# Hybrid attention block on one Trainium2 core: builds of x's combinations placed earlier, their writes placed behind the next weights, half of p and u kept in SBUF

## The chip, the cores and the metric

The kernel runs on one core of a Trainium2 chip. The metric is the device time of one execution in microseconds (us), the lower the better. The kernel before takes 834.61 us, the median of three runs (834.24, 834.61 and 836.61).

A core has five engines with their own instruction queues, each worked off in order: TensorE (PE, matmuls into PSUM; PEld are its weight loads), VectorE (DVE), ScalarE (ACT), GpSimd (POOL) and SyncE (SP, which here only issues DMAs). SBUF is the memory on the chip, HBM the one beside it.

## What is computed

x has 512 positions of 2048. One projection `h @ w_in` gives everything; two attention groups follow, and one output projection.

```python
h = _rmsnorm(x, norm_g[l])
proj = h @ w_in[l]
(qa, kca, vca, ksa, vsa, kwa, vwa, za, ga, qb, kb, vb, zb) = jnp.split(proj, offsets, axis=-1)
kc = _compress(_rope(_heads(kca, N_KV_A, HEAD_DIM_A)), cmp_k_pos[l], cmp_k_w1[l], cmp_k_w2[l])
vc = _compress(_heads(vca, N_KV_A, HEAD_DIM_A), cmp_v_pos[l], cmp_v_w1[l], cmp_v_w2[l])
...
o_a = gates[..., 0:1] * o_cmp + gates[..., 1:2] * o_sel + gates[..., 2:3] * o_win
y_a = o_a.reshape(B, S, WIDTH_A) * jax.nn.silu(za)
...
x = x + jnp.concatenate([y_a, y_b], axis=-1) @ w_out[l]
return _rmsnorm(x, final_g)
```

Group A has 8 heads of 128 on two key heads, with a compressed, a selected and a window branch; `_compress` takes blocks of 32 positions, adds a position table and runs a two-layer network over each block. Group B has 16 heads of 64 with a window and sinks.

## The kernel before, in words

Every float32 operand is split in a high part (ACT, a copy to fp32r) and a low part (DVE, the rest), and every product is three matmuls, high x high, high x low, low x high (`mm3`, L111 to L114). x stays in SBUF so split (xh, xl: 16 row tiles of 128 x 512).

Weights come in units of 512 KB or less: `load_unit` (L80) issues the load on SP into one of three buffers (raw0 to raw2; the compression weights cw have two of their own), ACT makes whi (L88), DVE wlo (L89), each in a ring of three. A load waits for the wlo three units back, a split for PE's last use three units back.

A planner of the build, with its own model of times, orders each engine's queue; `tc.issue_after(...)` in the source ties an instruction behind another one, such as the last wlo (`last["lo"]`) or the last load of weights (`last["dma"]`).

The stages, in order of time:

1. Start to 52 us: the first half of w0 (keys and values to be compressed), x loaded and split beside it.
2. 52 to 96: the second w0 loop (L291), 8 units of 24 matmuls. Beside it DVE scales the results (`kv_evac`, L199), and makes the blocks to be compressed (`blocks_part`, L210: ff on DVE, L214; high part on ACT, L215; low part on DVE, L216), which go to two tiles F0 and F1.
3. 96 to 126: the w1s loop (L324), 8 times 24 matmuls of w1s (`tok_chunk`) and 8 that compress keys with F0 and a unit of cw (`compress_unit`).
4. 126 to about 176: the w2s loop (L361), the same with 408 columns and F1 for values. `k_evac` (L312) finishes two of the keys in each of these loops, `v_evac` (L333) the values behind them.
5. The q tile and then the z tile of head 0 (`proj`, L369, 48 matmuls each), the evacuation of values and gates (L385 to L396), the compressed values VC (L397 to L409), then `p0.close()` (L410): the memory of the first stages, s0, s0b and rawc, goes to the pool wk of the heads (among it raw3, a fourth buffer for weights, and the tile that q is evacuated to).
6. To about 480: heads 0 to 7 of group A. From head 1 on q and z are made as a pair (`pair`, L614) by Strassen's scheme on 2 x 2 blocks, seven products of 24 matmuls of 256 columns in place of eight. The weights come in four quarters (wq) and are added on DVE (L624). On x's side the scheme needs combinations of its quarters.
7. Then group B, and the output projection.

The combinations of x are made once. Eight times `build` (L267, for the pair of row tiles m) takes two rows of x that `rows(m)` (L262) has loaded anew, combines their quarters (one ACT and four DVE steps, L272 to L276), and splits four forms f (four ACT, four DVE steps, L279 and L280): f = 0 is p, 1 is u, 2 is q, 3 replaces a quarter of x. All go to HBM, to fd, with one 1 MB write for each m (L282). SP issues it where it stands in the queue, and waits there for the build. The rows stand in one buffer of two halves, stage[0], the forms in stage[1]; both lie in the memory of the values (V), and from m = 4 on in that of F0 (`both`, L341).

One build is in the second w0 loop (behind unit 6), three in the w1s loop (0, 2, 5), four in the w2s loop (1, 2, 4, 6). `forms_back` (L584) loads it all back behind the first quarters of wq: eight loads for the tiles pu0 to pu7 (p and u, high and low, m below 4 and from 4), four that swap forms f = 3 into the even row tiles of x (`swap_x`; the old content was copied to xd at L303), four for f = 2 into the places of group 1's keys and values, which wait in HBM (Kd, Vd).

Of the kernel before, what the change touches and what calls it, by code (L numbers as in the profile page):

```python
# [34 lines left out]
def hybrid_block(ctx, tc, xT, xtm, w0, w1s, w2s, wz, wq, wkb, wo0, wos, cw1, cw2, cpos, rope, tabs, sinks, gT, fg, out):  # L35
# [27 lines left out]
    fd = dram("fd", 4, 2, P, KT // 2, 256)  # L63
# [41 lines left out]
    stage = [kv.tile([P, 2048], F32, name=f"st{e}", tag=f"V{e}") for e in "HL"]  # L105
# [15 lines left out]

    p0 = ExitStack()
    s0 = p0.enter_context(sb("s0"))
    vbs = s0.tile([P, NQ, P], F32, name="vbs")
# [33 lines left out]
    sqa = s0.tile([P, S], F32, name="sqa")  # L158
# [36 lines left out]
    kvts = [s0.tile([P, 2, S + 16], F32, name=f"kvt{b}") for b in range(2)]  # L195
# [11 lines left out]
    def blocks_tile(b):  # L207
        return s0.tile([P, 32, P], F32R, name=f"F{b}", tag=f"F{b}")

    def blocks_part(Fb, b, g, half):  # L210
        ff = tmp("ff").rearrange("p (a b) -> p a b", b=32)
        js = slice(half * 16, half * 16 + 16)
        src = kvts[b][:, g, half * 16:half * 16 + S].rearrange("p (b j) -> p j b", j=16)
        dve.tensor_tensor(out=ff, in0=src, in1=pos[:, b, js].unsqueeze(2).to_broadcast([P, 16, 32]), op=ALU.add)  # L214
        act.activation(Fb[:, js, g * 32:g * 32 + 32], ff, AF.Copy)  # L215
        dve.tensor_tensor(out=Fb[:, js, 64 + g * 32:96 + g * 32], in0=ff,  # L216
                          in1=Fb[:, js, g * 32:g * 32 + 32].bitcast(F32), op=ALU.subtract)

    def compress_unit(Fb, b, u, acc):
        hi, lo = load_unit(cw1[:, b, u], 1024, rawc)  # L220
        for j in range(4):
            jj = 4 * u + j
            cs = slice(j * 256, j * 256 + 256)
            pe.matmul(acc[:, 0:256], Fb[:, jj, :], hi[:, cs], start=jj == 0, stop=False)
            pe.matmul(acc[:, 0:256], Fb[:, jj, :], lo[:, cs], start=False, stop=jj == 31)
# [33 lines left out]
    even = [x.rearrange("p (m e) s -> p e m s", e=2)[:, 0, :, 0:256].bitcast(F32) for x in (xh, xl)]  # L259
    todo = []  # L260

    def rows(m):  # L262
        xr = stage[0][:, (m % 2) * 1024:(m % 2) * 1024 + 1024].rearrange("p (e s) -> p e s", e=2)
        nc.sync.dma_start(xr, xT[:, 2 * m:2 * m + 2, :])
        todo.append((m, xr, stage[1].rearrange("p (f c) -> p f c", f=8)))

    def build():  # L267
        m, xr, ft = todo.pop(0)
        ge, go = [gt[:, 2 * m + e:2 * m + e + 1] for e in range(2)]
        a11, a21, a12, a22 = xr[:, 0, H0], xr[:, 0, H1], xr[:, 1, H0], xr[:, 1, H1]  # L270
        with tc.issue_after(last["lo"]), tc.issue_after(last["hi"]):
# [5 lines left out]
            for f, (src, scale) in enumerate(((a11, 1.0), (a12, -1.0), (a21, ge), (a22, 1.0))):  # L277
                hi, lo = [ft[:, 2 * f + e, :].bitcast(F32R) for e in range(2)]
# [8 lines left out]
    bp = [lambda Fb=Fb, b=b, g=g, half=half: blocks_part(Fb, b, g, half)  # L287
          for b, Fb in enumerate((F0, F1)) for half in range(2) for g in range(2)]
    work = [kv[:1], kv[1:2], kv[2:], bp[0:2], bp[2:4], bp[4:5], bp[5:7], bp[7:]]
    acc1 = [bank(4 + i) for i in range(4)]  # L290
    for u in range(KT // 2):  # L291
# [12 lines left out]
        if u == 6:  # L304
            build()
# [34 lines left out]
    VH, VL = [kvp.tile([P, 2, NQ, 2, P], F32R, name=f"V{e}", tag=f"V{e}") for e in "HL"]  # L340
    both = s0.tile([P, 4096], F32, name="both", tag="F0")  # L341
    stage[:] = both[:, 0:2048], both[:, 2048:4096]
    with tc.issue_after(last["dma"]):
        rows(4)
        rows(5)
# [10 lines left out]

    for t in range(NQ):
# [11 lines left out]
    def proj(src, odd_first=False):  # L369
        ps = psp.tile([P, S], F32, name="pj", tag="pj")  # L370
        ready = []
        for u in range(2):
            ready.append(load_unit(src[:, u], 1024))
            ks = range(8 * u, 8 * u + 8)
            if odd_first:
                ks = [k for par in (1, 0) for k in range(par, KT, 2)] if u else []
            for k in ks:
                hi, lo = ready[k // 8]
                js = slice((k % 8) * P, (k % 8) * P + P)
                mm3(ps, hi[:, js], lo[:, js], xh[:, k, :], xl[:, k, :], k == (1 if odd_first else 0),  # L380
                    k == (KT - 2 if odd_first else KT - 1))
        return ps

    q0 = proj(wz[0])
    for t in range(NQ):  # L385
        v_evac(t, 1, sacc2[t])
        act.activation(vbs[:, t, :], sacc2[t][:, 256:384], AF.Copy, scale=rstd[:, t:t + 1])
        dve.tensor_scalar(gates[:, t, :], sacc2[t][:, 384:408], rstd[:, t:t + 1], None, op0=ALU.mult)
    for e in range(2):
        nc.sync.dma_start(Kd[e], (KH, KL)[e][1].bitcast(F32))  # L390
        nc.sync.dma_start(Vd[e], (VH, VL)[e][:, 1].rearrange("p t w c -> p (t w c)").bitcast(F32))
# [875 lines left out]
```

## Time and profile before

| | us |
|---|---|
| median of three runs | 834.61 |
| the profiled execution | 838.46 |
| its span, first to last instruction | 836.7 |
| PE busy | 815.8 |
| DVE busy | 665.9 |
| ACT busy | 486.4 |
| POOL busy | 86.8 |

The granted clock of TensorE is 0.997 on the mean. The DMA engines move 132.49 MB, at a mean of 158 GB/s. An instruction counts as busy from start to end, and PE's matmuls overlap: one starts before the last one's results are written. So idle time between matmuls is real, while a busy PE may still be slower than it could be. In a timeline the bracket behind a row has the idle time of the engine just before it, and the instruction or DMA whose end released it. Times within the span are counted from its start.

### The profile page before, as it was taken

To read this page: it belongs to the slowest core of one execution; us is meant where nothing else is said; L and a number is where in the kernel's file an instruction comes from. 1 tells how busy PE (TensorE), PEld (TensorE's weight loads), DVE (VectorE), ACT (ScalarE), POOL (GpSimd) and SP (SyncE) were. 2 spreads that over 40 slices of the span, in tenths; PEclk is the share of its full clock that TensorE was granted. 3 is DMA by queue.
4 is the path that set the end of the run, shared out by engine and by line. 5 is a ranking of instruction groups with operands and counts; after the bars stand their busy time and mean duration, and the time that the engine had idled before them with its cause. 6 is when DMAs were issued, how large, how long until landed. Compare 5 with 4: busy or idle time off the path is not lost.

```text
span 836.7 us, 14143 instructions
## 1 busy us (share of the span) xinstructions
PE 815.8 (98%) x5278; PEld 740.7 (89%) x5278; DVE 665.9 (80%) x1303; ACT 486.4 (58%) x1026; POOL 86.8 (10%) x69
## 2 busy tenths in 40 slices
PE   9999998998999999999999999999999999999996
PEld 8788898987999999999988888888888788999996
DVE  7869686866798989899866688887677798777895
ACT  6635457553668859676765365544543748443545
POOL 4500001011011011001111121011011000000000
PEclk9999999999999999999999999999999999999998
DMA  9682788894921323432732422231223127796835
GB/s 323 207 286 76 237 263 286 281 343 171 379 65 51 115 66 108 158 105 92 227 107 76 126 89 63 65 101 52 76 76 99 53 78 257 206 259 182 255 74 201
DMA packets 54164, 132.49 MB, mean 158 GB/s; under 512 B 4944, under 2 KB 19280, under 8 KB 54096
## 3 DMA queue, kind: packets, MB, share of 16 engines
q1 hardware_dynamic: 52080, 124.78, 45.0%
q0 software_dynamic: 1728, 6.29, 4.3%
q8 instruction: 41, 0.67, 0.3%
q10 hardware_dynamic: 288, 0.52, 0.2%
q14 instruction: 27, 0.22, 0.1%
HBM read 112.41 MB, written 19.17 MB: 157 GB/s over the span
## 4 chain that ended last, share of the span: by engine, by line
PE 67%; DVE 3%; DMA 3%; issue 1%; ACT 1%; SPq 0%; POOL 0%; DVEq 0%; ACTq 0%
PE pj L112 14%; PE pj L113 14%; PE pj L114 14%; PE oa L113 4%; PE oa L112 4%; PE oa L114 4%; PE sp L499 3%; PE tp L537 2%; PE tp L803 1%; DMA ch<-wos 1%; DMA late<-xtm 1%; PE spb L768 1%; PE spb L769 1%; PE op L544 1%; PE op L543 1%
## 5 line engine op out<-in xcount | busy, mean ns | idle before, releaser
L112 PE MATMUL pj<-xh,whi 128*128 128x512 f32 (+1 forms) x560 | 196.5, 351 | 3.4 <-DVE t L119 1.6
L114 PE MATMUL pj<-xh,wlo 128*128 128x512 f32 (+1 forms) x560 | 196.1, 350 | 0.6 <-DVE wlo L576 0.6
L113 PE MATMUL pj<-xl,whi 128*128 128x512 f32 (+1 forms) x560 | 195.8, 350 | 0.0
L89 DVE TENSOR_TENSOR wlo<-raw,whi 128x1024 fp32r<-128x1024 f32 (+2 forms) x102 | 115.2, 1130 | 36.0 <-ACT whi L88 35.2
L88 ACT ACTIVATE whi<-raw 128x1024 fp32r<-128x1024 f32 (+1 forms) x101 | 95.1, 944 | 74.0 <-PE pj L113 24.5
L112 PEld LDWEIGHTS pj<-xh,whi 128*128 128x128 f32 x560 | 105.5, 188 | 16.8 <-issue 2.0
L114 PEld LDWEIGHTS pj<-xh,wlo 128*128 128x128 f32 x560 | 105.4, 188 | 14.0 <-DVE wlo L576 0.8
L113 PEld LDWEIGHTS pj<-xl,whi 128*128 128x128 f32 x560 | 105.5, 188 | 13.6 <-issue 0.7
L576 DVE TENSOR_TENSOR wlo<-raw,whi 128x1024 fp32r<-128x1024 f32 x49 | 61.5, 1259 | 14.1 <-ACT whi L575 13.8
L575 ACT ACTIVATE whi<-raw 128x1024 fp32r<-128x1024 f32 x49 | 51.7, 1058 | 35.7 <-PE pj L113 12.7
L112 PE MATMUL oa<-whi,yh 128*128 128x256 f32 (+1 forms) x168 | 50.7, 303 | 0.6 <-ACT yh L857 0.6
L113 PE MATMUL oa<-wlo,yh 128*128 128x256 f32 (+1 forms) x168 | 51.1, 304 | 0.1
L114 PE MATMUL oa<-whi,yl 128*128 128x256 f32 (+1 forms) x168 | 50.3, 302 | 0.0
L782 ACT ACTIVATE ttb<-ttb,mnb 128x256 f32<-128x256 f32 (+1 forms) x64 | 30.1, 471 | 25.9 <-DVE mnb L775 25.4
L468 ACT ACTIVATE ph<-tp 128x512 fp32r<-128x512 f32 x56 | 32.4, 592 | 21.6 <-PE tp L537 14.9
L469 DVE TENSOR_TENSOR pl<-tp,ph 128x512 fp32r<-128x512 f32 x56 | 37.9, 684 | 6.1 <-ACT ph L468 6.1
L113 PE MATMUL bank<-wlo,xh 128*128 128x256 f32 (+1 forms) x128 | 40.5, 318 | 0.9 <-DVE wlo L89 0.9
L114 PE MATMUL bank<-whi,xl 128*128 128x256 f32 (+1 forms) x128 | 40.0, 314 | 0.0
L112 PE MATMUL bank<-whi,xh 128*128 128x256 f32 (+1 forms) x128 | 36.3, 317 | 2.5 <-ACT whi L88 2.5
L427 POOL TENSOR_TENSOR t<-t,t 128x512 f32<-128x512 f32 x9 | 19.3, 2147 | 182.5 <-DVE t L119 135.2
L112 PE MATMUL bank<-xh,whi 128*128 128x512 f32 x96 | 37.3, 399 | 0.0
L113 PE MATMUL bank<-xl,whi 128*128 128x512 f32 x96 | 37.1, 391 | 0.0
(350 smaller groups left out, 2214.3 us busy)
## 6 DMA issues: line engine op xcount, KB each, us to landing
raw<-wz SPq DMA_DIRECT2D x36, 512.0 KB, 3.8
raw<-wq SPq DMA_DIRECT2D x28, 512.0 KB, 3.9
raw<-cw SPq DMA_DIRECT2D x16, 512.0 KB, 5.2
raw<-wos SPq DMA_DIRECT2D x12, 512.0 KB, 4.7
rw<-wos SPq DMA_DIRECT2D x10, 512.0 KB, 6.1
xr<-xT SPq DMA_DIRECT2D x16, 256.0 KB, 5.0
raw<-w SPq DMA_DIRECT2D x8, 512.0 KB, 4.2
fd<-stL SPq DMA_DIRECT2D x4, 1024.0 KB, 5.5
```

Of the source, the lines that this page charges most:

```text
L88: last["hi"] = act.activation(hi[:, :width], rw[:, :width], AF.Copy).ins
L89: last["lo"] = dve.tensor_tensor(out=lo[:, :width], in0=rw[:, :width], in1=hi[:, :width].bitcast(F32), op=ALU.subtract).ins
L112: pe.matmul(ps, ah, bh, start=first, stop=False, skip_group_check=go_on)
L113: pe.matmul(ps, ah, bl, start=False, stop=False, skip_group_check=go_on)
L114: recent["mm"] = pe.matmul(ps, al, bh, start=False, stop=last, skip_group_check=go_on).ins
L427: pool.tensor_tensor(out=t1, in0=t1, in1=t2, op=ALU.add)
L468: act.activation(ph, tp, AF.Copy)
L469: dve.tensor_tensor(out=pl, in0=tp, in1=ph.bitcast(F32), op=ALU.subtract)
L499: pe.matmul(sp[:, a:b], qq[:, qs], kk[0][:, ko:ko + b - a], start=pi == 0, stop=pi == 2)
L575: act.activation(hi, src, AF.Copy)
L576: last["lo"] = dve.tensor_tensor(out=lo, in0=src, in1=hi.bitcast(F32), op=ALU.subtract).ins
L782: act.activation(tv, tv, AF.Exp, bias=mn[:, e, v:v + 1], scale=-1.0, accum_out=dn[:, e, v:v + 1])
```

## The change

- Where builds stand: behind units 3, 5 and 7 of the second w0 loop, 3 of the w1s loop, and 2, 3, 5 and 6 of the w2s loop. The first rows are loaded behind units 0 and 1 of the second w0 loop; xd is copied behind unit 6 in place of 5.
- `build` no longer issues its write. It leaves a function, which is called at later units, issues the write behind the last load of weights, and then loads rows m + 2.
- Buffers: rows of m below 4 stand in the memory of V's high part (two tiles), their forms in one tile ft in that of V's low part. From m = 4 rows stand in kvt0 and kvt1, which have been read by then.
- For m from 4 the high and low parts of p and u are made right in the odd tiles pu1, pu3, pu5 and pu7 and stay there; forms 2 and 3 go to HBM from small tiles (fq, fv, sq, sqa) as two writes of 256 KB (fw). fd is half as large. fv shares its tile with vbs.
- F0 and F1 become four tiles each, in the pool yp, in the places of the odd and the even tiles of pu. A part of them takes half as many positions for both key heads: two DVE adds of 256 columns in place of one of 512 for each 512 that ACT and DVE split.
- The values, their writes, the compressed hidden layer and VC are called within the q tile's projection. `proj` loads both units ahead; z takes the even row tiles of x first.
- `forms_back` loads four tiles of pu between the first and the other quarters of wq, then forms 2 and 3.
- k_evac stands behind units 1 and 5 (w1s) and 1 and 4 (w2s) in place of 1, 4 and 3, 5. `last["jj"]` is taken from the instruction behind.

```diff
-    stage = [kv.tile([P, 2048], F32, name=f"st{e}", tag=f"V{e}") for e in "HL"]
+    stage = kv.tile([P, 2, 2, S], F32, name="rows", tag="VH")
...
-        return s0.tile([P, 32, P], F32R, name=f"F{b}", tag=f"F{b}")
+        return [yp.tile([P, 8, P], F32R, name=f"F{b}{i}", tag=f"yp{2 * i + 1 - b}") for i in range(4)]
...
+        for g in range(2):
+            src = kvts[b][:, g, i // 2 * 16:i // 2 * 16 + S].rearrange("p (b j) -> p j b", j=16)
+            src = src[:, i % 2 * 8:i % 2 * 8 + 8, :]
+            dve.tensor_tensor(out=ff[:, g], in0=src, in1=pos[:, b, i * 8:i * 8 + 8].unsqueeze(2).to_broadcast([P, 8, 32]),
+                              op=ALU.add)
+        act.activation(hi, ff, AF.Copy)
+        dve.tensor_tensor(out=lo, in0=ff, in1=hi.bitcast(F32), op=ALU.subtract)
...
     def build():
-        m, xr, ft = todo.pop(0)
+        m, xr = todo.pop(0)
+        if m < 4:
+            ft = kvp.tile([P, 8, 256], F32, name="ft", tag="VL")
+            words = [[ft[:, 2 * f + e, :].bitcast(F32R) for e in range(2)] for f in range(4)]
+            out = [(fd.rearrange("f e p m c -> p (f e) m c")[:, :, m, :], ft)]
+        else:
+            if m % 2:
+                two = tmp("fq"), s0.tile([P, NQ, P], F32, name="fv", tag="vbs").rearrange("p a b -> p (a b)")
+            else:
+                two = (s0b.tile([P, S], F32, name="sq", tag="sq", bufs=1),
+                       s0.tile([P, S], F32, name="sqa", tag="sqa"))
+            two = [t.rearrange("p (e c) -> p e c", e=2) for t in two]
+            words = [[pu[2 * (2 * f + e) + 1][:, m - 4, :] for e in range(2)] for f in range(2)]
+            words += [[t[:, e, :].bitcast(F32R) for e in range(2)] for t in two]
+            out = [(fw[f].rearrange("e p m c -> p e m c")[:, :, m - 4, :], t) for f, t in enumerate(two)]
...
-            nc.sync.dma_start(fd.rearrange("f e p m c -> p (f e) m c")[:, :, m, :], ft)
-        if m % 4 < 2:
-            rows(m + 2)
+        def write():
+            with tc.issue_after(last["dma"]):
+                for dst, src in out:
+                    nc.sync.dma_start(dst, src)
+                if m + 2 < 8:
+                    rows(m + 2)
+        writes.append(write)
...
-        if u == 3:
+        if u < 2:
             with tc.issue_after(last["dma"]):
-                rows(0)
-                rows(1)
-        if u == 5:
+                rows(u)
+        if u == 6:
             with tc.issue_after(last["dma"]):
                 for e in range(2):
                     nc.sync.dma_start(xd[e], even[e])
-        if u == 6:
+        if u in (5, 7):
+            writes.pop(0)()
+        if u in (3, 5, 7):
             build()
...
-        if u in (1, 4):
+        if u in (1, 5):
             with tc.issue_after(last["lo"]):
-                k_evac(0, u // 4)
-        if u in (0, 2, 5):
+                k_evac(0, u // 5)
+        if u in (2, 6):
+            writes.pop(0)()
+        if u == 3:
             build()
...
-        if u in (3, 5):
+        if u in (1, 4):
             with tc.issue_after(last["lo"]):
-                k_evac(1, u // 5)
-        if u in (1, 2, 4, 6):
+                k_evac(1, u // 4)
+        if u in (4, 5, 7):
+            writes.pop(0)()
+        if u in (2, 3, 5, 6):
             build()
...
+    q0 = proj(wz[0], jobs={1: lambda: writes.pop(0)(), 4: words_out,
+                           8: lambda: hidden.append(compress_hidden(1, vacc)), 12: compressed_values})
     p0.close()
...
-    pu = [yp.tile([P, 4, 256], F32R, name=f"pu{j}", tag=f"yp{j}") for j in range(8)]
+    for j in (0, 2, 4, 6):
+        pu[j] = yp.tile([P, 4, 256], F32R, name=f"pu{j}", tag=f"yp{j}")
...
-            st = z_evac(proj(wz[8]))
-            first = [load_quarter(wq[0], c, quarter) for c, quarter in zip(tags, (3, 0, 2, 1))]
-            forms_back()
+            st = z_evac(proj(wz[8], 0))
+            lows, highs = slice(0, 4), slice(4, 8)
+            first = []
+            with tc.issue_after(last["dma"]):
+                first.append(load_quarter(wq[0], tags[0], 3))
+                forms_back(0, lows)
+                forms_back(1, lows)
+            for c, quarter in zip(tags[1:], (0, 2, 1)):
+                with tc.issue_after(last["dma"]):
+                    first.append(load_quarter(wq[0], c, quarter))
+            with tc.issue_after(last["dma"]):
+                for f in (2, 3):
+                    forms_back(f, lows)
+                    forms_back(f, highs)
```

More of the change, by code (lines that the diff above doesn't have):

```diff
@@ L193, in hybrid_block @@
     nc.sync.dma_start(pos, cpos)
-    kvts = [s0.tile([P, 2, S + 16], F32, name=f"kvt{b}") for b in range(2)]
+    kvts = [s0.tile([P, 2, S + 16], F32, name=f"kvt{b}", tag=f"kvt{b}") for b in range(2)]
     for b in range(2):
@@ L338, in v_evac @@
         pool.tensor_tensor(out=VL[:, :, t, w, :], in0=vg, in1=VH[:, :, t, w, :].bitcast(F32), op=ALU.subtract)
[L340 to L345, printed above, removed]
+    for j in (1, 3, 5, 7):
+        pu[j] = yp.tile([P, 4, 256], F32R, name=f"pu{j}", tag=f"yp{j}")
     sl = compress_hidden(0, kacc)
@@ L355, in hybrid_block @@
                           op=ALU.subtract)
+    VH, VL = [kvp.tile([P, 2, NQ, 2, P], F32R, name=f"V{e}", tag=f"V{e}") for e in "HL"]
     for t in range(NQ):
@@ L384, in hybrid_block @@
[L384 to L391, printed above, removed]
-    nc.sync.dma_start(vbd, vbs)
-    act.activation(gates, gates, AF.Tanh, scale=0.5)
```

140 lines of the change are left out of this document (79 added, 61 removed).

## The prediction

> **What bounds the kernel now.** First the page's head and busy time, then the table by stretches (us from the span's start; span, then busy time and count of each engine).
>
> ```profile
> span 836.7 us, 14143 instructions
> ...
> PE 815.8 (98%) x5278; PEld 740.7 (89%) x5278; DVE 665.9 (80%) x1303; ACT 486.4 (58%) x1026; POOL 86.8 (10%) x69
> ```
> ```profile
> 52.00:96.00 44.00, 44.00 (x194) 36.18 (x195) 37.77 (x54) 17.73 (x28) 0.00 (x0) 1.00 0.54 174
> 96.00:126.00 30.00, 29.83 (x249) 29.20 (x248) 23.86 (x40) 16.27 (x26) 0.00 (x0) 1.00 0.83 267
> 126.00:176.00 50.00, 46.39 (x271) 45.10 (x270) 39.87 (x64) 30.76 (x56) 3.00 (x4) 1.00 0.85 293
> 176.00:202.00 26.00, 24.40 (x116) 19.98 (x114) 14.41 (x26) 10.01 (x23) 3.54 (x4) 1.00 0.60 207
> 202.00:215.00 13.00, 11.24 (x87) 10.55 (x88) 8.35 (x20) 7.91 (x19) 3.10 (x2) 1.00 0.98 361
> 215.00:480.00 265.00, 261.96 (x1964) 249.41 (x1963) 222.89 (x469) 181.13 (x431) 27.45 (x18) 1.00 0.38 123
> 480.00:837.00 357.00, 347.36 (x2169) 308.59 (x2168) 282.15 (x593) 189.22 (x394) 27.50 (x21) 0.99 0.44 128
> ```
>
> TensorE (PE) bounds it. The change removes no matmul, so it can only return PE's idle time: 50.00 - 46.39 = 3.61 us in the second token loop (w2s) and up to the q tile, 1.60 in the q and z tiles, 1.76 at the start of the first head pair. That is 6.97 us in all, and no more than that is to be had where the change works. The heads behind it (215 to 480) idle for 3.04 us. From about 480 the two built programs issue the same 2170 matmuls in the same order. The third view is PE's timeline, with only the rows that have an idle time before them (in brackets, with its releaser):
>
> ```profile
> 126.99 0.64 PE L112 MATMUL bank<-whi,xh 128*128 128x408 f32 x2 [0.48 <-ACT whi L88]
> 130.96 0.39 PE L225 MATMUL bank<-wlo,F 128*128 128x256 f32 x1 [0.27 <-DVE wlo L89]
> 140.41 1.01 PE L112 MATMUL bank<-whi,xh 128*128 128x408 f32 x4 [2.07 <-ACT whi L88]
> 155.12 0.46 PE L113 MATMUL bank<-wlo,xh 128*128 128x408 f32 x1 [0.53 <-DVE wlo L89]
> 166.39 0.46 PE L113 MATMUL bank<-wlo,xh 128*128 128x408 f32 x1 [0.26 <-DVE wlo L89]
> 201.94 0.36 PE L112 MATMUL pj<-xh,whi 128*128 128x256 f32 x1 [1.60 <-DVE t L119]
> 205.50 0.38 PE L112 MATMUL pj<-pu,whi 128*128 128x256 f32 x1 [0.22 <-DVE zr L417]
> 206.39 0.39 PE L113 MATMUL pj<-pu,whi 128*128 128x256 f32 x1 [0.52 <-DMA pu<-fd]
> 214.15 0.39 PE L112 MATMUL pj<-pu,whi 128*128 128x256 f32 x1 [1.03 <-DVE mn L505]
> ```
>
> These nine rows are 6.98 us: all of it.
>
> **The change part by part.** *Builds moved up.* The longest of these waits has its cause on ScalarE (ACT):
>
> ```profile
> 136.46 0.72 ACT L272 ACTIVATE both<-both,gt 128x512 f32<-128x512 f32 x1 [1.84 <-DMA both<-xT]
> ...
> 139.49 0.87 ACT L88 ACTIVATE whi<-raw 128x816 fp32r<-128x816 f32 x1
> ```
>
> A build of x's combinations waits for its rows of x, and the split of the next weights (L88), which PE needs at 138.3, stands behind it. In the new order three builds stand in the second w0 loop, one in the w1s loop and four in the w2s loop, each behind weights that come first, and their rows are loaded well ahead: the 2.07 us go. The 0.53 and 0.26 us are wlo splits on VectorE (DVE) behind the evacuation of k and a build; the new order keeps one of the two evacuations clear of the builds, and there is no later weight or row in their place, so I count both as gone. The 0.48 and 0.27 us at the loop's start are weights that landed late behind a 1 MB write of forms (fd). That write is still there, and a 512 KB load of rows now stands ahead of it, but ACT and DVE have no build there: I count half as gone, 0.38 us.
>
> What the move costs lies between 52 and 96, where PE never idles. PE's start of this loop, and DVE rows of before:
>
> ```profile
> 52.06 0.48 PE L112 MATMUL bank<-xh,whi 128*128 128x512 f32 x1
> ```
> ```profile
> 63.49 1.23 DVE L89 TENSOR_TENSOR wlo<-raw,whi 128x1024 fp32r<-128x1024 f32 x1
> ...
> 65.84 1.22 DVE L89 TENSOR_TENSOR wlo<-raw,whi 128x1024 fp32r<-128x1024 f32 x1
> 66.98 3.91 DVE L214 TENSOR_TENSOR ff<-kvt,pos 128x512 f32<-128x512 f32 x4
> ```
> ```profile
> L214 DVE TENSOR_TENSOR ff<-kvt,pos 128x512 f32<-128x512 f32 x8 | 8.0, 1038 | 0.0
> L216 DVE TENSOR_TENSOR F<-ff,F 128x512 fp32r<-128x512 f32 x8 | 5.4, 688 | 0.1
> ...
> L314 DVE TENSOR_TENSOR t<-t,t 128x512 f32<-128x512 f32 x4 | 2.7, 685 | 0.0
> ...
> L275 DVE SCALAR_TENSOR_TENSOR stH<-stH,gt 128x256 f32<-128x256 f32 x4 | 2.0, 488 | 0.1
> ...
> L276 DVE TENSOR_TENSOR stH<-stH 128x256 f32<-128x256 f32 x4 | 1.7, 426 | 0.0
> ```
>
> From 63.49 DVE now has, up to the split that the loop's seventh unit of weights needs: four such splits (4.9 us), two kvt sums like L314 (1.4), 14 halves of L214 (half of 1038 ns each, 7.3), five of L216 (3.4), nine steps of builds at about 0.46 (4.1). By durations that ends at 63.49 + 21.1 = 84.6; since each row starts about 0.08 before the last one's end (65.84 + 1.22 against 66.98), and there are 34, it is nearer 81.9. PE comes to that unit at 52.06 + 6 x 24 x 44.00/194 = 84.7. So DVE is on time by 0.1 to 2.8 us, and the step costs nothing; PE's own work on the units before is the cover, and past it each microsecond of DVE is one of PE. Splitting L214 in two adds eight instructions, each at the difference of the rows, 2 x 426 - 685 = 0.17 us, 1.3 us in all, which that margin holds. The copy of x's even rows (xd, 2 MB) moves behind the seventh unit's load and ahead of the eighth's; that one goes when the fifth unit's split has ended, near 67, and PE needs it at 90.1, so it has 16 us for 2.5 MB beyond the splits.
>
> *Writes behind weights, one buffer for forms.* The new ft is one tile. So ACT's first forms of the next build wait until the write of the last has landed, and on DVE the low parts of that build stand ahead of the next wlo. From the page's list of DMA issues (last number: median us to landing):
>
> ```profile
> fd<-stL SPq DMA_DIRECT2D x4, 1024.0 KB, 5.5
> fd<-both SPq DMA_DIRECT2D x4, 1024.0 KB, 6.7
> pu<-fd SPq DMA_DIRECT2D x8, 512.0 KB, 9.8
> ```
>
> From the view of all instructions with fd (its last line), and from PE's timeline the first use of that wlo:
>
> ```profile
> DMA to landing us min/median/max: 5.3/8.9/12.2
> ```
> ```profile
> 99.92 0.28 PE L113 MATMUL bank<-wlo,xh 128*128 128x256 f32 x1
> ```
>
> The first write can go at 83.3 (SP's queue puts it behind the weights that wait for the split at 82 to 83) and lands at 88.8. The second build's forms follow, four ACT steps and four on DVE, 2.4 us; the second write goes at 91.2 and lands at 96.7; the third build's forms hold DVE until about 98.9, and the split of the second w1s unit ends at 99.6. PE needs it at 99.9. SP waits for the builds as well: behind the second and the third write stand loads of cw and w1s, which go between 92 and 102; PE comes to the first of them two units of w1s and cw later, after 64 matmuls of 0.12 (29.83/249), at 107.6. With a landing of 5.3 there is 0.7 us to spare, with 9.8 it is 2 x 4.3 - 0.3 = 8.3 us late. I take 5.5 to 6, the rows of this very write, and a cost of 0.3 us; 0 and 8.3 are the ends. [...] The rows show 5.5 and more, and they decide.
>
> *Half of p and u kept, compressed values earlier.* Behind the z tile, SP, the queue of DMAs, and DVE stood like this:
>
> ```profile
> SPq L611 <- DVE VC L409: 13.7, 1, 13.7
> ```
> ```profile
> 184.54 14.48 SPq L611 DMA_DIRECT2D raw<-wq  x2
> 199.07 4.28 SPq L589 DMA_DIRECT2D pu<-fd  x8
> ```
> ```profile
> 197.36 1.18 DVE L409 TENSOR_TENSOR VC<-vc,VC 32x128 fp32r<-32x128 f32 x4
> ...
> 201.11 0.68 DVE L119 TENSOR_TENSOR t<-pj,sinA 64x512 f32<-64x512 f32 x1
> ```
>
> SP waits 13.7 us for the compressed values (VC), which free the memory of the first stage; only then go the fourth quarter of wq and the eight loads of p and u. DVE's evacuation of q stands behind VC too, and PE's first product waits for it: 1.60, then 0.52 for pu itself, and 0.22 and 1.03 for DVE work that this made late. In the new order VC's last matmuls stand 54 behind q's start; 42 of the 96 of q and z, 42 x 44.00/194 = 9.5 us, still follow, and VC with the evacuation of q takes DVE 1.18 + 3 x 0.68 = 3.2. The four loads of pu that are left stand ahead of wq; the other four need none. So these 3.37 us go (1.60 + 0.22 + 0.52 + 1.03). What is late next is the swap of x's even rows, queued behind VC: z ends at 200.34 less the 3.2 us above, 197.1, so the loads go near 191, and 4 MB at the 361 GB/s of the stretch 202 to 215 are 11.6 us, up to 203. The product that reads them stands 112 matmuls behind z's end, at 29.83/249 = 0.12 us 13 us, so at 210. ACT has one new wait:
>
> ```profile
> 182.19 1.06 ACT L88 ACTIVATE whi<-raw 128x1024 fp32r<-128x1024 f32 x1 [0.59 <-PE pj L113]
> ```
>
> vbs shares its tile with the last form, whose write must land first; vbs, the gates and this split stand behind it. The form is made with the split of q's first unit, so its write goes near 170 and lands near 176; the split waits for PE to free its buffer anyway, here at 182.2, then at 179. That covers it by 3 us; past that each microsecond costs one.
>
> *Heads.* The scheduler reorders heads 1 to 7 with it. Nothing shows which way: between all their idle time gone (-3.04) and as much again (+3.04); I take 0.
>
> Sum: 2.07 + 0.53 + 0.26 + 0.38 + 3.37 = 6.6 gone, 0.3 added, so 6.3 us. The profiled execution took 838.46 (span 836.7), and would take 832.2. The median shown is 834.61, 3.85 less; I move it by the same: **828.3 us**.
>
> **The rivals.**
> *Given back in part.* The loads at the w2s loop stay late and the new order of the heads costs up to 3.04: only 2.07 and 1.60, whose causes are plainly gone, come through: 834.61 - 3.67 + 0 to 3.04 = 830.9 to 834. For it: DMA is at 0.83 to 0.85 between 96 and 176. Against: 2 MB of writes less pass there, and 2 MB of loads less behind it.
> *Slower: the single buffer.* If the writes of forms land like pu<-fd did in a crowd (9.8), PE stands 8.3 us at 100, and wlo again behind the third write: 834.61 - 6.3 - 0.3 + 8.3 = 836.3, and 837 to 840 with 1 to 4 us there too. It decides once a write needs over 9 us: 2 x (9 - 5.5) - 0.3 is the 6.6 us gained. For it speaks that DMA is at 0.83 there; against, that the fd rows of the same stretch are at 5.5. [...]
> *It doesn't do what it says.* If the 2.07 and 1.60 only move (the build then waits for its landed write, PE for another DVE step), the time stays at 832.5 to 837. For it: DVE is at 0.80 of the w2s loop (39.87 of 50). Against: in the new order of SP's queue the rows of each build of that loop go two or more loads of weights ahead of it.
>
> **How the numbers follow.** Forecast, 824.6 (all 6.97 and the heads' 3.04 gone) to 830.9: 0.62. In part, 830.9 to 834: 0.18, half of it under 832.1. No effect, 832.5 to 837: 0.11. Slower, 836 to 840: 0.09. The range 824.0 to 834.0 holds the first two and the nearer part of the third. A measurement here tells 0.3%, 2.5 us, from no change. Faster than 832.1: 0.62 + 0.09 = 0.71. Within: 0.09 + 0.11 = 0.20. Slower than 837.1: 0.09.
>
> **What would show it.** Right: no idle row of 0.3 us or more on PE between 131 and 215; VC ended and q evacuated ahead of z's end; the loads of pu landed ahead of it. Wrong: PE waiting at 99 to 106 for wlo or whi while ACT waits for fd (the single buffer); PE idle near 85 or 90 (DVE late in the w0 loop); vbs waiting on ACT beyond 179; more than 3 us of new idle time between 215 and 480.

## The result, and the profile after

The changed kernel takes 829.19 us (median of 7 runs, 828.32 to 832.83), the kernel before, run beside it, 835.05 (7 runs, 834.09 to 837.42). The ratio is 0.9935, with a 95% interval of 0.9914 to 0.9957: 5.9 us faster, where 6.3 was forecast. The profiled execution took 829.19, with a span of 827.4 at the same granted clock, 0.997.

The head of its page, and the stretches that answer to those of before (span; busy time and count of PE, PEld, DVE, ACT and POOL; granted clock; DMA share; GB/s):

```profile
span 827.4 us, 14161 instructions
...
PE 811.5 (98%) x5278; PEld 735.6 (89%) x5278; DVE 662.1 (80%) x1311; ACT 485.6 (59%) x1026; POOL 89.3 (11%) x69
```
```profile
52.00:96.00 44.00, 44.00 (x198) 36.26 (x197) 40.43 (x66) 18.96 (x30) 0.00 (x0) 1.00 0.54 175
96.00:126.00 30.00, 30.00 (x248) 29.41 (x248) 22.41 (x35) 15.22 (x25) 0.00 (x0) 1.00 0.91 310
126.00:174.00 48.00, 46.31 (x273) 45.10 (x272) 38.66 (x63) 32.52 (x59) 4.82 (x5) 1.00 0.76 248
174.00:198.00 24.00, 24.00 (x115) 19.99 (x114) 11.82 (x24) 10.07 (x22) 6.18 (x6) 1.00 0.90 333
198.00:212.00 14.00, 14.00 (x115) 13.81 (x114) 12.52 (x27) 8.28 (x20) 0.00 (x0) 1.00 0.74 251
212.00:475.00 263.00, 259.53 (x1936) 245.79 (x1936) 219.33 (x465) 179.02 (x428) 28.58 (x18) 1.00 0.33 106
475.00:827.00 352.00, 344.03 (x2171) 305.32 (x2169) 281.91 (x593) 189.07 (x394) 27.66 (x21) 0.99 0.43 131
```

PE never idles in the q and z tiles and at the start of the first pair any more (24.00 of 24, 14.00 of 14). From 126 to 174 it lacks 1.69, and 3.47 in the heads. All that is left of the nine idle rows of before, 96 to 212, is four rows in the first part of the w2s loop:

```profile
127.10 0.39 PE L228 MATMUL bank<-whi,F 128*128 128x256 f32 x1 [0.39 <-ACT whi L89]
127.87 0.64 PE L113 MATMUL bank<-whi,xh 128*128 128x408 f32 x2 [0.39 <-ACT whi L89]
131.96 0.64 PE L113 MATMUL bank<-whi,xh 128*128 128x408 f32 x2 [0.46 <-ACT whi L89]
139.75 1.08 PE L113 MATMUL bank<-whi,xh 128*128 128x408 f32 x4 [0.46 <-ACT whi L89]
```

The first two are a load that lands late: ACT stands idle for it, and then has two splits to make at once.

```profile
125.99 1.83 ACT L89 ACTIVATE whi<-raw 128x1024 fp32r<-128x1024 f32 x2 [4.50 <-DMA raw<-cw]
```

The span is 9.3 us shorter than that of before (836.7), the medians differ by 5.9. Read by stages, from the starts of four matmuls in each timeline: up to the first w1s matmul the changed kernel is 0.6 later (96.74 against 96.11; in the first 52 us, in unchanged code, it idles 0.28 for the high part of x at 5.12 and 0.68 for a split of weights at 25.75, where the kernel before idles 0.17 for a split); from there to the first pair's first matmul (198.24, before 201.94) it gains 4.3; from there to the last 2170 matmuls (474.97, before 479.58) 0.9; and in these 2170, the same in the same order, another 4.7. The last is taken up at the end.

### The profile page after: what moved, and what is told of

The parts are those of the page before. It is cut to its first block, busy times and chain, and to the rows that moved or that the text cites. A ratio compares the mean times of both kernels' runs of the same rounds, so it can differ in the third digit from the quotient of the medians.

```text
span 827.4 us, 14161 instructions
## 1 busy us (share of the span) xinstructions
PE 811.5 (98%) x5278; PEld 735.6 (89%) x5278; DVE 662.1 (80%) x1311; ACT 485.6 (59%) x1026; POOL 89.3 (11%) x69
## 4 chain that ended last, share of the span: by engine, by line
PE 84%; DVE 6%; DMA 5%; issue 2%; ACT 2%; SPq 0%; DVEq 0%; ACTq 0%; POOLq 0%
PE pj L115 16%; PE pj L113 15%; PE pj L114 15%; PE bank L115 4%; PE bank L113 4%; PE oa L114 4%; PE oa L113 4%; PE oa L115 3%; PE sp L539 3%; PE bank L114 3%; PE tp L855 2%; DMA rw<-wos 1%; PE tp L577 1%; DMA xr<-xT 1%; DMA raw<-cw 1%
```

## The experiments

All twelve in one table. A is the time from the first w1s matmul to the first pair's first matmul, B from there to the last 2170 matmuls, both from the timelines, in us. The ratio is to the kernel before, run beside each.

```
run                          A       B       median  ratio, 95% interval
before                     105.83  277.64
before again (e4)          105.73  277.65   835.56  1.0000  0.9983-1.0017
changed                    101.50  276.73   829.19  0.9935  0.9914-0.9957
changed again (e12)        101.43  276.85   829.08  0.9922  0.9898-0.9946
e1  values late            101.61  279.32   832.68  0.9970  0.9954-0.9985
e2  values early alone     103.81  274.50   829.31  0.9929  0.9909-0.9949
e3  halves reloaded        104.99  280.98   838.23  1.0021  1.0002-1.0039
e5  e2, builds later       101.37  274.27   829.23  0.9901  0.9882-0.9919
e6  marker back            101.00  282.35   835.34  0.9994  0.9977-1.0012
e7  last write later       100.79  276.72   831.22  0.9925  0.9906-0.9944
e8  write twice            108.58  276.95   837.46  1.0030  1.0009-1.0050
e9  write beside           104.17  276.79   831.88  0.9963  0.9947-0.9978
e10 marker alone           105.57  279.58   839.47  1.0055  1.0034-1.0075
e11 e5 with marker         101.08  277.70   832.59  0.9966  0.9947-0.9984
```

### One part undone, and the same part alone (e1, e2)

```diff
-    q0 = proj(wz[0], jobs={1: lambda: writes.pop(0)(), 4: words_out,
-                           8: lambda: hidden.append(compress_hidden(1, vacc)), 12: compressed_values})
+    q0 = proj(wz[0], jobs={1: lambda: writes.pop(0)()})
+    words_out()
+    hidden.append(compress_hidden(1, vacc))
+    compressed_values()
```

> The changed kernel with one part undone: the words of v and vb, the gates and the compressed values stand behind the whole of q's projection again, as before; the builds, the writes and the kept halves of p and u stay. Theory of the prediction: SP's queue and DVE wait for the compressed values again, so PE's idle rows at the start of the first head pair come back (1.60 before q's evacuation, then up to 1.77 more): 1.6 to 3.4 us slower than the changed kernel, 830.8 to 832.6. Rival: the kept halves alone did it, since half of p and u need no load any more; then at most the wait for DVE's zr and pu of 0.2 to 0.5 comes back: 829.2 to 829.7.

e2 is the reverse: these functions and the `jobs` of `proj` in the kernel before (there `proj` loads both units of q ahead, and the transfers of `words_out` stand behind the last load of weights), and nothing else of the change.

> The kernel before with one part of the change alone: the words of v, the gates, the second E2 product and the compressed values are put between q's matmuls; builds, rows, writes and all eight loads of p and u as before. Theory of the prediction: the 3.37 us at the start of the first head pair go by this part alone, 835.05 - 3.4 = 831.7; the eight loads of p and u and the 4 MB of x that follow take 2 MB more than in the changed kernel, which at 361 GB/s is 5.8 us, so x may be 1 us late: 831.2 to 832.7. Rival: without the earlier builds the last form is written too late and the loads stay late; then at most the 1.60 of DVE's evacuation goes: 833.4 to 835.

e2 has no idle row between 180 and 220, where before has 3.36 us, and reaches 0.9929: the same as the whole change, and more than the theory's 3.4 us. That the idle rows go by this part alone holds. A gains 2.0 and B 3.1, more than the 1.77 of the first pair, so a new order of the heads has a part in it. It has all eight loads of p and u, and they cost nothing; in its queue the quarters of wq stand ahead of them. Its one long wait is that of the build in the w2s loop:

```profile
140.09 1.01 PE L112 MATMUL bank<-whi,xh 128*128 128x408 f32 x4 [1.83 <-ACT whi L88]
```

e1 loses 2.0 us up to the last 2170 matmuls (476.94 against 474.97), and by the ratios 2.9: as much as the theory said, but not where it said. A is the same. On DVE nothing stands between VC and the evacuation of q now, where before had a sum of weights of 1.22 us, and the evacuation ends 0.3 us before PE comes. The loss is in B:

```profile
201.50 0.39 PE L113 MATMUL pj<-pu,whi 128*128 128x256 f32 x1 [0.44 <-DVE zr L460]
...
233.77 0.38 PE L113 MATMUL pj<-xh,whi 128*128 128x256 f32 x1 [1.20 <-ACT t L683]
```

The first row is the theory's wait for zr, 0.44 of its 1.77. The second is not one that the theory named: ACT evacuates t there behind a split of weights that waits 1.65 us for PE, and what put it there is not shown. So how much late values cost at the first pair depends on the order that DVE happens to have there; 3.4 was right for the order of before.

### The kept halves (e3)

```diff
         def write():
...
+                if m == 7:
+                    for j in range(4):
+                        nc.sync.dma_start(fp[j], pu[2 * j + 1].bitcast(F32))
...
     def forms_back(f, ms):
...
                 nc.sync.dma_start(pu[4 * f + 2 * e].bitcast(F32), fd[f, e])
+                nc.sync.dma_start(pu[4 * f + 2 * e + 1].bitcast(F32), fp[2 * f + e])
```

> The changed kernel, and beside it the four kept halves of p and u are also written to HBM behind the last form and read back in front of the first pair, so 2 MB more go each way, as before. Theory: keeping the halves is what leaves room for the swap of x's even rows. That landed at 206.5 in the changed kernel and is needed about 13 us behind the first pair's first matmul at 198.2, at 211. 2 MB more to read are 5.8 us at 361 GB/s, so it lands at 212 and PE idles by 1 us; with the 2 MB of writes ahead of it too, at 218, 7 us: 830 to 836. Rival: the halves are worth nothing, since the transfers have room: 829.2 and no new idle row between 195 and 215.

Slower by 0.9% than the changed kernel (1.0021 against 0.9935), but the theory named the wrong transfer. A is 3.5 longer, B 4.3 (in B PE's clock falls twice, at 203 and 394; see the end). The swap of x is not what comes late; the weights are, since in the changed order the loads of p and u stand ahead of the quarters of wq. ACT of e3, and then PE:

```profile
191.92 1.06 ACT L620 ACTIVATE whi<-raw 128x1024 fp32r<-128x1024 f32 x1 [0.44 <-DMA raw<-wq]
196.83 1.06 ACT L620 ACTIVATE whi<-raw 128x1024 fp32r<-128x1024 f32 x1 [3.85 <-DMA raw<-wq]
```
```profile
201.29 0.36 PE L114 MATMUL pj<-xh,whi 128*128 128x256 f32 x1 [2.74 <-DVE t L121]
```

The evacuation of q stands on DVE behind the split of those weights, at 199 where the changed kernel has it at 190. Beside e2, where all eight loads stand behind the weights and cost nothing, this means that the halves must be kept only because loads were moved ahead of the weights.

### The builds of the w2s loop alone (e5)

e2, and in the w2s loop:

```diff
-        if u in (3, 5):
+        if u in (1, 4):
             with tc.issue_after(last["lo"]):
-                k_evac(1, u // 5)
-        if u in (1, 2, 4, 6):
+                k_evac(1, u // 4)
+        if u in (2, 3, 5, 6):
             build()
```

> The kernel before with the values put within q's projection (as in the run e2), and beside it the four builds of the w2s loop one unit of weights later (2, 3, 5, 6 in place of 1, 2, 4, 6) and the two evacuations of k at 1 and 4, as in the changed kernel; rows, writes and all eight loads of p and u as before. Theory: the wait of the first of these builds for its rows of x (PE idle 1.83 at 140.1 in e2) is a matter of how far the rows are loaded ahead, so one unit, some 6 us, is enough: the row goes, and with e2's 829.3 that gives 827.5. Rival: the wait only moves, to the next build, whose write must have left the one buffer before, or to the weights that now stand behind the later write of the last forms: 829 to 832.

```profile
139.98 1.01 PE L112 MATMUL bank<-whi,xh 128*128 128x408 f32 x4 [0.74 <-ACT whi L88]
```

The long wait fell from 1.83 to 0.74 and the row at the entrance grew from 0.21 to 0.49. A is 101.37, 2.4 less than in e2 (the 1.6 of it that idle rows don't explain are told at the end) and that of the whole change. The median doesn't show it by itself (829.23 against 829.31, on different chips); the ratio does, 0.9901, the lowest of all. So two edits, the values within q and the builds of one loop a unit later, do what all of the change does up to the first pair, and lose less in the heads. Builds in an earlier loop, writes behind weights and kept halves bring nothing beyond them in these runs. That e5 beats the changed kernel rests on 2.3 us at the last 2170 matmuls (472.68 against 474.97); the intervals of the ratios still overlap.

### The line in the heads (e6, e10, e11)

The diff has one line in `pair` that the prediction did not price: what the next pair's first sum of weights is issued behind. e6 puts it back:

```diff
-        plus(jj, jj, pb[:, H1])
-        last["jj"] = plus(zr, zr, rstdb, ALU.mult)
+        last["jj"] = plus(jj, jj, pb[:, H1])
+        plus(zr, zr, rstdb, ALU.mult)
```

> The changed kernel with one line of a head pair as before: what the next pair's first sum of weights is issued behind is again the sum into jj and not the product with rstdb that follows it. Up to 198.2, the first pair, nothing differs. Theory: this line is what the heads lost. From the first pair's first matmul to the last 2170 matmuls the changed kernel takes 276.7 us with 3.5 idle, e2 with the old line 274.5 with 2.4 idle: 1 to 2 us faster, 827.2 to 828.2. Rival: every new order of the heads moves these idle rows about, this line among other things: the same sum of 3 to 4 us in other places, 828.7 to 829.7.

Both theories fall: B is 282.35, 5.6 us longer, and the ratio 0.9994. Without this line the whole change would have been worth nothing that the ratio can tell (0.9977 to 1.0012). Of the 5.6, 3.7 are idle rows and 1.7 a fall of PE's clock at 265.8 in this profile (see the end). DVE and PE in e6:

```profile
257.31 1.23 DVE L558 TENSOR_TENSOR dn<-dn,gates 128x6 f32<-128x6 f32 x1
258.46 0.41 DVE L665 TENSOR_TENSOR zr<-zr,pj 128x256 f32<-128x256 f32 x1
```
```profile
259.01 0.36 PE L113 MATMUL pj<-pu,whi 128*128 128x256 f32 x1 [1.20 <-DVE zr L665]
...
355.55 0.36 PE L113 MATMUL pj<-pu,whi 128*128 128x256 f32 x1 [1.20 <-DVE zr L665]
```

The sum that frees PE's bank stands behind a step of the softmax (dn), here and again near 355. Next the line by itself, in the kernel before (e10) and in e5 (e11):

> The kernel before with one line changed: in a head pair, what the next pair's first sum of weights is issued behind is the product with rstdb and not the sum into jj ahead of it, as in the changed kernel. Up to 202 nothing differs. Theory: the line is worth something by itself. Without it the changed kernel took 282.4 us from the first pair's first matmul to the last 2170 matmuls, with it 276.7; here this stretch (277.6, idle 3.04) loses most of the waits for zr behind that sum (0.62 at 356.7) and for t (1.48 at 391.6): 1 to 3 us faster, ratio 0.996 to 0.999. Rival: it only changes which order the scheduler finds, and the sign is open: within 1 us, or slower by up to 5.

> The kernel of the run e5 (before, with the values within q's projection and the four builds of the w2s loop one unit later) with the marker line of the changed kernel in the head pairs. Up to 198 nothing differs from e5. Theory: the line takes the waits for zr and t out of the heads, where e5 has 2.27 us idle in 274.3: 1 to 2 us faster than e5, a ratio of 0.988 to 0.989, the fastest so far. Rival: the line matters only with the transfers and the order of the changed kernel, and here it makes another order: 0.990 or more.

In both it makes things worse: e10 is at 1.0055 (its trace gives 1.5 us of that up to the last 2170 matmuls, 481.05 against 479.58, and B 1.9; where the rest of the 0.55% is stays open), e11 at 0.9966 against e5's 0.9901, with B longer by 3.4. The same wait turns up, in e10:

```profile
387.50 0.36 PE L112 MATMUL pj<-pu,whi 128*128 128x256 f32 x1 [1.21 <-DVE zr L624]
...
393.46 0.39 PE L543 MATMUL op<-ph,VH 128*128 128x256 f32 x1 [1.12 <-ACT ph L468]
```

The line has no worth of its own. It decides which order the planner finds, and its sign turns with what else is changed. For one order B repeats: 276.7 to 277.0 in the changed kernel twice, e7, e8 and e9, 277.64 and 277.65 in before. From order to order it goes from 274.3 to 282.4, falls of the clock in e3 and e6 included.

### The entrance of the w2s loop (e7)

```diff
-                if m + 2 < 8:
+                if m + 2 < 8 and m not in (3,):
                     rows(m + 2)
...
-        if u in (2, 6):
+        if u in (2, 7):
             writes.pop(0)()
         if u == 3:
             build()
+        if u == 4:
+            with tc.issue_after(last["dma"]):
+                rows(5)
```

> The changed kernel with two transfers off the entrance of the w2s loop: the write of the forms m = 3 goes one unit of weights later, behind the last weights of the w1s loop, and the 512 KB of rows for m = 5, which stood behind that write, go two units earlier. Theory: the four rows of 0.39 to 0.46 us that PE still idles at 127 to 140 (1.70 in all) come from these 1.5 MB, queued among the weights between 114 and 118, which then land 7 to 9 us after issue; they fall to 0.3 or less, 827.5 to 827.9. Rival: the DMA engines are busy for 0.91 of 96 to 126 anyway, so something lands late whatever the order: 1.2 or more stays, 828.7 to 829.7.

```profile
130.82 0.39 PE L229 MATMUL bank<-wlo,F 128*128 128x256 f32 x1 [0.86 <-DVE wlo L90]
139.15 1.01 PE L113 MATMUL bank<-whi,xh 128*128 128x408 f32 x4 [0.99 <-ACT whi L89]
```

The rows at 127 went, two later ones took their place, 1.85 in all; A is 0.7 shorter, the ratio the same. The edit was weak: the write left at 117.84 in place of 115.68. The row near 139 is no late load: ACT makes that split at 138.23, behind an evacuation of k that it waited 3.20 us for, so the theory put too much down to the two transfers. Whether these 1.7 us can be had by order alone stays open.

### The single buffer (e8, e9)

```diff
                 for dst, src in out:
-                    nc.sync.dma_start(dst, src)
+                    wrote = nc.sync.dma_start(dst, src).ins
+                if m < 2:
+                    with tc.issue_after(wrote):
+                        nc.sync.dma_start(f2.rearrange("f e p m c -> p (f e) m c")[:, :, m, :], src)
```

f2 is memory that nobody reads; the views, which leave out numbers in names, call it f. In e9 the second transfer's source is `xh[:, 0:4, :]`, of the same size and shape.

> The changed kernel, and behind the first and the second write of forms the same buffer is written a second time, to memory that nobody reads: 1 MB more each time, and the buffer is free only when both have landed. Theory (the prediction's rival of the single buffer): the first two writes landed 5.5 and 5.3 us after issue in the changed kernel, and the split of the second w1s unit then ended at 100.06, 0.49 us before PE came to it at 100.55. 1 MB more at 310 to 361 GB/s is 2.9 to 3.4 us for each, so PE idles 2 x 3.1 - 0.5 = 5.8 us (5.3 to 6.3) between 100 and 107, and the time is 5 to 7 us above the changed kernel's, a ratio of 1.000 to 1.002 to before. Rival: the wait for the buffer isn't on the path, since ACT and DVE have other work: under 1 us idle there, ratio 0.993 to 0.995.

> As the run with the doubled write, but the second 1 MB behind the first and the second write of forms is read from x's words, which nobody changes before 190: the same traffic at the same places of the queue, and the buffer of forms is not held by it. Theory: what costs in the doubled write is the buffer and not the traffic, so PE idles under 1 us between 100 and 107 here; the weights behind it land some 3 us later, and the entrance of the w2s loop may idle by up to 1 us more: ratio 0.9935 to 0.995. Rival: the traffic does it, since DMA is at 0.91 from 96 to 126: as slow as with the doubled write, 0.998 to 1.002.

ACT and PE of e8:

```profile
91.68 0.72 ACT L302 ACTIVATE ft<-rows 128x256 fp32r<-128x256 f32 x2 [6.16 <-DMA f<-ft]
...
103.12 0.72 ACT L302 ACTIVATE ft<-rows 128x256 fp32r<-128x256 f32 x2 [6.62 <-DMA f<-ft]
```
```profile
105.54 0.39 PE L229 MATMUL bank<-whi,F 128*128 128x256 f32 x1 [3.01 <-ACT whi L90]
```

The two writes of a form now hold the buffer for 8.7 us (82.89 to 91.57) and 8.5 (94.56 to 103.01). A is 7.1 longer than in the changed kernel, the ratio 1.0030. With the same traffic beside the buffer (e9) A is 2.7 longer, and 0.9963:

```profile
101.13 0.38 PE L114 MATMUL bank<-whi,xh 128*128 128x256 f32 x1 [0.82 <-ACT whi L90]
...
114.04 0.51 PE L114 MATMUL bank<-whi,xh 128*128 128x256 f32 x2 [0.75 <-ACT whi L90]
```

So the traffic costs more than the theory gave it (2.7, not up to 1), and the ratio of e9 lies between theory and rival. The buffer is left with 7.1 - 2.7 = 4.4 where 5.8 was expected, and only 1.5 of that is idle time of 96 to 126 (4.0 us in e8, 2.5 in e9). The rest is a fall of PE's clock in e8, behind the wait of 3.01 (see the end); e9's wait of 0.82 had none behind it.

### The same kernels again (e4, e12)

> The kernel before, unchanged, for a second profile. The profiled execution of before and of after differ by 9.3 us, the medians by 5.86. In the last 130 us, whose code and order are the same, a 256-column matmul took 117.7 ns in before's profile and 113.3 in after's. Theory: that is a difference between executions and not between kernels, so this profile, or the one after it, shows 113.3 with before's code too, and the span comes to 832; the times of the rounds spread by some 2.5 us. Rival: the change sets it; then 117.7 again and a span of 836 to 837.

> The changed kernel, unchanged, for a second ratio beside that of e5 (0.9901, 0.9882 to 0.9919) and a second profile. Theory on the ratio: e5 reaches the last 2170 matmuls at 472.7 and the changed kernel at 475.0, so e5 is the faster one by 2.3 us: the changed kernel comes to 0.993 again, its two intervals centred above 0.992. Rival: e5 only had the better rounds, and this one comes to 0.990 to 0.991. Theory on the last 130 us: a 256-column matmul takes 113.3 or 117.7 ns by how the execution came into this part and not by the kernel, so 117.7 here would show it at one and the same kernel; 113.3 again would leave it open, since both profiles of before show 117.7. The stretch from the first pair's first matmul to the last 2170 matmuls, 276.7 us, is set by the order of the instructions and comes out the same within 0.3.

Both repeat their A and B, and each its own step in the last part, so these two profiles leave e4's rival standing; e7 and e10 speak against it (see the end). The ratio 0.9922 is on the first theory's side only just, so it doesn't settle how far e5 is ahead.

## Why the prediction came out

*Values within q (3.37).* Right, and shown by e2: alone it takes all 3.36 us away. The kept halves and the loads moved ahead of wq, which the prediction counted into the cause, were not needed: e2 has neither. In the changed kernel VC ends and q is evacuated ahead of z's end, as the prediction asked:

```profile
189.02 1.18 DVE L446 TENSOR_TENSOR VC<-vc,VC 32x128 fp32r<-32x128 f32 x4 [0.38 <-ACT VC L444]
...
191.80 0.68 DVE L120 TENSOR_TENSOR t<-pj,sinA 64x512 f32<-64x512 f32 x1
```

The four loads of pu landed by 183.8. The swap of x landed at 206.5, not near 203, and nobody waited for it.

*The wait for vbs.* It was said to be covered until 179. ACT waited 0.25 us for the last form's write and was done at 178.9; the split behind it waited for PE anyway:

```profile
177.74 1.14 ACT L418 ACTIVATE vbs<-bank,rstd 128x128 f32<-128x128 f32 x4 [0.25 <-DMA fw<-fv]
```

*Builds (2.07, 0.53, 0.26).* The rows' wait went, and the two behind k with it. But 0.46 stays at 139.75, a split of weights. e5 shows that the place of the builds in the w2s loop is enough for that. The 0.53 and 0.26 are not in every execution of the kernel before: e4, whose clock fell at 141, has no such rows.

*The entrance (0.38).* This is the step that failed: "ACT and DVE have no build there: I count half as gone". The builds were not what these rows waited for. Of 0.75 us, 0.37 was to be left; three rows of 1.24 are, and with the 0.46 above the loop idles for 1.70 ("no idle row of 0.3 us or more on PE between 131 and 215" was to be the sign). The first two rows are a load that lands late: ACT stood idle for 4.5 us until a unit of cw, behind the 1 MB write, had landed at 125.88. The other two aren't. ACT splits for them at 131.02 and 138.82, and by the order of the queue those loads had landed at 126.92 and 129.16:

```profile
131.02 0.89 ACT L89 ACTIVATE whi<-raw 128x816 fp32r<-128x816 f32 x1
...
138.82 0.88 ACT L89 ACTIVATE whi<-raw 128x816 fp32r<-128x816 f32 x1 [2.82 <-PE bank L228]
```

At 131.02 ACT is behind with its work since 125.99, evacuations of values among it. At 138.82 it waits for PE to free the place in the ring of three, and PE then waits for the split; this row is 0.46 in e1, e3, e6, e8 and e12 as well. DMA rose from 0.83 to 0.91 of 96 to 126; whether the added load of rows and the 1 MB write are to blame for the late load, or the mere amount of traffic, is not shown: e7 moved them too little.

*DVE in the second w0 loop.* On time by 0.1 to 2.8 us, it said. The split for the seventh unit ends at 83.60, PE comes to it at 85.74: 2.1 us.

*The single buffer (0.3, with 8.3 as the bad end).* It cost nothing. The second w1s split was to end at 99.6 with PE at 99.9; it ended at 100.06 with PE at 100.55:

```profile
97.39 0.42 ACT L301 ACTIVATE ft<-rows 128x256 fp32r<-128x256 f32 x1 [4.54 <-DMA fd<-ft]
```
```profile
99.37 0.69 DVE L90 TENSOR_TENSOR wlo<-raw,whi 128x512 fp32r<-128x512 f32 x1
```
```profile
100.55 0.28 PE L114 MATMUL bank<-wlo,xh 128*128 128x256 f32 x1
```

The first two writes landed after 5.5 and 5.3 us, as the rows had it. e8 shows the mechanism of the rival at work, at 8.5 us of buffer time.

*Heads (0).* The size of this step is where luck was. Net, B gives back 0.9 of the 1.77 us that the first pair gains, within the range that the prediction kept. But the net hides two terms that it did not see: 5.6 us that the marker line saves in this order, and 4.7 that the rest of the change costs in B without it (282.35 against 277.64; 1.7 of that is the fall of PE's clock in e6's profile). "Nothing shows which way" was true; ±3.04, taken from idle time that was there, was too narrow for a reorder, which can add waits of its own: e6 has B 4.7 us above before.

The sum: 4.3 us of A (4.54 forecast, with 0.3 of cost), 0.9 of B (1.77 forecast), less 0.6 ahead of both: 4.6 us at the last 2170 matmuls, beside 5.9 in the medians. The difference is within the interval of the ratio (3.6 to 7.2 us).

## What to carry to other kernels

Look for the smallest part of a change that explains its gain: here two of the edits did what the whole did, and others only served each other (loads moved ahead of weights made it necessary to keep half of them). Where a planner orders the queues, price every line of the diff that gives it a tie, also the harmless one; a new order of an untouched stage moved its time in the traces by up to 8 us here, more than any wait that was aimed at. A buffer that a DMA must release cost nothing here where the landing plus the work behind it fit the gap (landings of 5.5 and 5.3 us), and 4.4 us where it was held for 8.7 and 8.5 (e8 against e9); measure the landing in that stretch, and double it once to see what it decides.

## What the runs showed of the hardware

*Behind some short waits PE ran at half its clock.* In e2 PE idled 1.83 us up to 140.09, and from 141.0 on ran for 3.4 us at half its clock. The same stretch in e2 and in before, where the wait was 2.07:

```profile
141.00:144.50 3.50, 3.50 (x12) 3.45 (x11) 1.31 (x5) 1.68 (x2) 0.00 (x0) 0.52 0.70 175
```
```profile
141.00:144.50 3.50, 3.50 (x21) 3.50 (x20) 1.96 (x5) 2.28 (x5) 0.00 (x0) 1.00 0.59 135
```

12 matmuls in place of 21, with PE busy throughout. In e4, the kernel before again, the clock fell at the same place, behind a wait of 1.79, and in e10 behind one of 1.89. In e3 it fell behind 2.74 at 201.29 and behind 1.13 at 393.34, in e6 behind 1.14 at 264.98. In e8 it fell for 6.8 us behind the 3.01, and those 3.4 us of lost work with the 4.0 of idle time are about the 7.1 by which A grew there. So a wait of some 2 us is worth up to 3.7 (an estimate: the wait and half of 3.4), and not in every execution; the prediction, from a profile without such a fall, counted the bare 2.07. That the idle time brings the fall is read from where the falls stand, each within 2 us of the end of such a wait (0.9 in e2, 0.8 in e6); no run changed the wait alone, and e6 has the same 1.14 once more, at 361.51, with no fall behind it. The granted clock is 0.52 in e2 (141.00 to 144.50) and in e8 (106.50 to 113.50), 0.53 in e4 (141.00 to 144.50); what sets the length of a fall, 3.4 us and in e8 6.8, is not shown.

*Matmuls of 256 columns at two steps.* 60 us of the output projection in after's profile and in before's, the same code in the same order, without an idle row:

```profile
740.00:800.00 60.00, 60.00 (x531) 60.00 (x531) 50.22 (x57) 30.19 (x39) 5.22 (x6) 1.00 0.75 203
```
```profile
748.00:808.00 60.00, 60.00 (x511) 60.00 (x511) 49.42 (x56) 29.46 (x39) 5.23 (x6) 1.00 0.74 198
```

113.0 ns a matmul against 117.4, at a granted clock of 1.00. Of the 4.7 us in the last 2170 matmuls, this step makes 3.2, over some 730 matmuls. Another 1.7 are two stops of PE in before, at 723.23 and 727.23, for weights of the output projection that land late (ACT, then PE, of before); after in turn has a stop of 0.3 near 804 that before hasn't.

```profile
720.85 1.06 ACT L861 ACTIVATE whi<-ch 128x1024 fp32r<-128x1024 f32 x1 [3.07 <-DMA ch<-wos]
```
```profile
727.23 0.39 PE L113 MATMUL oa<-wlo,uh 128*128 128x256 f32 x1 [1.01 <-DVE wlo L862]
```

The step isn't tied to the change: e10, before with one line changed, has the short step from 730 on, e7, the changed kernel with two transfers moved, the long one from the start of the part at 703. Nor is it shown to change from execution to execution of one kernel: both profiles of before have the long step, both of after the short one. The times leave room for it (e4's ten executions go from 833.43 to 838.99, the profiled one being the longest). Within an execution it changes both ways: from short to long between 718 and 728 in before, e2, e4 and e5 and at 797 in e3, from long to short between 722 and 730 in e6, e8 and e10. PE waits at the change for 1.01 us in before, 0.60 in e4 and 0.15 in e3, and not at all in e2. What holds it is open, and so is why the weights land later in before. With these 4.7 us the spans of the two profiles were 9.3 us apart, where the medians were 5.9.
